# Moving chunk 2's input and the norm weights from SyncE's DMA queue to ScalarE's in a one-core hybrid decoder layer

## The chip, the cores and the metric

The kernel runs on one core of one Trainium2 chip. The metric is the time of one execution on the device in microseconds (us), lower is better. Each engine of the core (TensorE or PE, VectorE or DVE, ScalarE or ACT, GpSimd or POOL, SyncE or SP) works through its own list of instructions in order; the lists meet through semaphores. A DMA is started by an instruction in the list of one engine.

## The reference

One layer of a decoder on 1024 prompt tokens and 64 sample tokens that share all weights, in float32:

```
x = x + 0.5 * rms(swiglu_1(rms(x, n1a)), n1b)      # up: 1024 -> 2 x 2816, down: 2816 -> 1024
z = rms(x, mxa) @ w_in
a = sliding-window attention with sinks;  b = short conv + gated DeltaNet, gated rms
m = (sigmoid(gA) * (a @ w_a) + sigmoid(gB) * (b @ w_b)) @ w_out
x = x + rms(m, mxb)
x = x + 0.5 * rms(swiglu_2(rms(x, n2a)), n2b)
rms(v, w) = v * rsqrt(mean(v * v) + 1e-6) * w
```

Only the first few tens of microseconds of the first SwiGLU matter here: `silu(h @ gate) * (h @ up)` with `h = rms(x, n1a)`.

## The kernel before

Everything lies feature-major: 1024 features are 8 tiles `k` of 128 partitions, tokens are columns. The 1088 tokens are cut into three chunks of 384, 384 and 320 columns; chunk 2 holds the last 256 prompt tokens and the 64 sample tokens. Every float32 matrix is split into a rounded high part and a remainder (names `h_` and `l_` for weights, `xuh`/`xul`, `xsh`/`xsl` for inputs), and a product is three matmuls: high by high (line 142), high by remainder (143), remainder by high (144). For a weight piece of 128x512 the high part is a cast on ScalarE (line 115), the remainder a subtraction on VectorE (line 116). Weight pieces arrive in buffers named `r_` (4 of them) and `q_` (3); a buffer is free again when VectorE has made the remainder.

The kernel begins with chunk 2 alone (`pass_a`): for hidden tiles f = 0, 1, 2, ... it multiplies by the gate and the up weight. `first()` loads the four weight pieces of f = 0 (`r_w`), each followed by a quarter of chunk 2's input (`load_x(2, ...)`, two tiles k: 128 x 640), then the identity and the ones (`eye1`). `make_xn` scales the input by the norm weight (`vec`) and splits it: `xuh` on ScalarE (line 202), `xul` on VectorE (line 203). The statistic of the norm (`stat(2)`, the function `rms`) runs beside it: squares on ScalarE (line 170), sums on VectorE (lines 172 and 175), a matmul with ones (line 179, tile `po`), then ScalarE and VectorE make the factor `r`. In group 0 (f = 0 to 3) the factor is applied behind the matmuls (lines 388 to 391); from group 1 on the matmuls read `xs`, which is scaled by it beforehand (`make_xnr`: line 215 on VectorE, 195 on ScalarE, 196 on VectorE). Between the hidden tiles, `input1` fetches chunks 0 and 1 and makes their statistics (`po_725` for chunk 0), and `ldd` fetches the down weights (`h_da`), whose products are added up in `ya` (lines 347 to 351).

The code is not the order of execution. A scheduler in the framework sorts the instructions of every engine when the kernel is built, by data dependences, by priorities (`high_priority` raises one) and by its own estimates of when data is there; what comes out is fixed and each engine then keeps it. So a DMA that moves to another engine's list can change the order of the rest. In the kernel before, every DMA is issued by SyncE.

Of the kernel before, what the change touches and what calls it, by code (L numbers as in the profile page):

```python
# [35 lines left out]
def body(ctx: ExitStack, tc: tile.TileContext, d):  # L36
    nc = tc.nc
# [8 lines left out]

    eye1 = cp.tile([P, 2 * P], F32, tag="eye1", name="eye1")
    vec = cp.tile([P, V_END], F32, tag="vec", name="vec")
    nc.sync.dma_start(vec, d["vec"])
    ident = eye1[:, 0:P]  # L50
    ones = eye1[:, P : 2 * P]

    def width(c):
        return CH[c][1] - CH[c][0]
# [13 lines left out]
    def whole(pool, c, name, dt=F32):  # L68
        return [pool.tile([P, 4, width(c)], dt, tag="big", name=f"{name}{c}_{j}") for j in range(2)]

    def at(t, k):
        return t[k // 4][:, k % 4, :]

    def pair(pool, c, name):
        return whole(pool, c, f"{name}h", F32R), whole(pool, c, f"{name}l", F32R)

    def f32(ap):
        return ap.bitcast(F32)
# [3 lines left out]
    def uid(s):  # L82
        cnt[0] += 1
        return f"{s}_{cnt[0]}"
# [25 lines left out]
    def raw(name):  # L110
        return wp.tile([P, 4, P], F32, tag="raw", name=f"r_{name}", bufs=4)

    def split_w(full, hi, lo):
        with tc.high_priority(offset=20000):
            nc.scalar.copy(hi, full)  # L115
            nc.vector.tensor_tensor(out=lo, in0=full, in1=f32(hi), op=ALU.subtract)
        return hi, lo

    def slot(name, pool=wp, tag="w"):
        return (  # L120
            pool.tile([P, 4, P], F32R, tag=f"{tag}h", name=f"h_{name}"),
            pool.tile([P, 4, P], F32R, tag=f"{tag}l", name=f"l_{name}"),
        )
# [40 lines left out]
    def rms(pool, src, n, dst, scale, urgent=False):  # L164

        t = pool.tile([P, 4, 384], F32, tag="big", name=uid("rms"))
        acc, sq = t[:, 0:2, :n], t[:, 2:4, :n]
        for k in range(0, KT, 2):
            for i in range(2):
                nc.scalar.activation((sq if k else acc)[:, i, :], src(k + i), AF.Square)  # L170
            if k:
                nc.vector.tensor_tensor(out=acc, in0=acc, in1=sq, op=ALU.add)
            yield
        one, ve = acc[:, 0, :], acc[:, 1, :]
        nc.vector.tensor_tensor(out=one, in0=one, in1=ve, op=ALU.add)
        yield
        ps = po_tile()
        with tc.high_priority(offset=4000 if urgent else 0):
            sums.append(nc.tensor.matmul(ps[:, :n], ones, one, start=True, stop=True))
        nc.scalar.activation(dst, ps[:, :n], AF.Abs_reciprocal_sqrt, scale=scale, bias=epsc)  # L180
        nc.scalar.activation(ve, ps[:, :n], AF.Identity, scale=scale, bias=epsc)
        newton(dst, ve, one)
        yield

    def drain(steps):
        for _ in steps:
            pass

    def take(steps, n):
        for _ in range(n):  # L190
            if next(steps, steps) is steps:
                return
# [5 lines left out]
    def make_xn(x, xn, wcol):  # L198
        xh, xl = xn
        for k in range(KT):  # L200
            wv = vec[:, wcol + k : wcol + k + 1]
            nc.scalar.activation(at(xh, k), at(x, k), AF.Copy, scale=wv)
            nc.vector.scalar_tensor_tensor(
                out=at(xl, k), in0=at(x, k), scalar=wv, in1=f32(at(xh, k)), op0=ALU.mult, op1=ALU.subtract
            )
            if k % 2:
                yield

    def make_xnr(x, xn, wcol, rr, c):

        xh, xl = xn
        n = width(c)
        for k in range(KT):
            t = t2()[:, :n]
            nc.vector.scalar_tensor_tensor(
                out=t, in0=at(x, k), scalar=wcol[:, k : k + 1], in1=rr, op0=ALU.mult, op1=ALU.mult
            )
            split(t, at(xh, k), at(xl, k))
            if k % 2:
                yield  # L220
# [25 lines left out]
    def spill(y, dst):  # L246
        for j in range(2):
            nc.sync.dma_start(dst[:, 4 * j : 4 * j + 4, :], y[j])

    def scaled(x, wcol, rr):  # L250

        for k in range(KT):
            nc.vector.scalar_tensor_tensor(
                out=at(x, k), in0=at(x, k), scalar=wcol[:, k : k + 1], in1=rr, op0=ALU.mult, op1=ALU.mult
            )
            if k % 2:
                yield
# [284 lines left out]
    def rtile(name, c):  # L542
        return cp.tile([P, width(c)], F32, tag=f"r{c}", name=f"{name}{c}")
# [3 lines left out]
    def unit(u, name):  # L547
        return load_w(win[u], name)
# [5 lines left out]
    with tc.tile_pool(name="f1", bufs=12, side="left", reuse_waits="tile") as big1, tc.tile_pool(  # L554
        name="d1", bufs=4, side="right", reuse_waits="tile"
    ) as dw1:
        r1 = [rtile("r1", c) for c in range(3)]
        x0 = [whole(xp, 0, "x0"), whole(xp, 1, "x0"), whole(big1, 2, "x0")]
        xu = pair(xp, 2, "xu")

        def load_x(c, k):
            nc.sync.dma_start(x0[c][k // 4][:, k % 4 : k % 4 + 2, :], d[f"x{c}"][:, k : k + 2, :])

        def stat(c):
            return rms(big1, lambda k: at(x0[c], k), width(c), r1[c], 1.0 / 1024.0, False)

        def first():
            ws = []
            for i in range(2):
                for w in range(2):  # L570
                    t = raw(f"w0{w}{i}")
                    nc.sync.dma_start(t, d["up1"][w * NFF][:, 4 * i : 4 * i + 4, :])
                    load_x(2, 4 * i + 2 * w)
                    ws.append(split_w(t, *slot(f"w0{w}{i}")))
            nc.sync.dma_start(eye1, d["eye1"])
            drain(make_xn(x0[2], xu, V_N1A))
            with tc.high_priority(offset=20000):
                drain(stat(2))
            return ws[0::2], ws[1::2]

        f1 = FFN(d["up1"], d["dn1"], Two(big1, dw1), "a")
        xs2 = []
        cx1 = {}

        def input1():
            for c in range(2):
                for k in range(0, KT, 2):
                    load_x(c, k)
                yield
                yield from stat(c)  # L590
                yield from scaled(x0[c], hn1, r1[c])
            yield from combine(big1, x0[0], x0[1], cx1)

        def xs1(g):
            if g == 1 and not xs2:
                xs2.append(pair(big1, 2, "xs"))
                drain(make_xnr(x0[2], xs2[0], hn1, r1[2], 2))
            return xs2[0] if g else xu

        xn2 = [None] * 3  # L600
        r2 = [None] * 3
        xd1 = [d[f"x{c}"] for c in range(3)]

        def again(src, wcol, rr):
            x = whole(xp, 2, uid("xk"))
            for j in range(2):
                nc.sync.dma_start(x[j], src[:, 4 * j : 4 * j + 4, :])
            xs = pair(xp, 2, uid("xk"))
            drain(make_xnr(x, xs, wcol, rr, 2))
            return xs  # L610

        def close1(c):
            y = f1.y[c]
            yield from post(big1, y, hv1, xd1, c, early=True)
            xn2[c] = pair(xp, c, "xb")
            r2[c] = rtile("r2", c)
            spill(y, xd[c])
            if c == 2:
                yield from make_xn(y, xn2[c], V_MXA)
                yield from rms(big1, lambda k: at(y, k), width(c), r2[c], 1.0 / 1024.0)  # L620
            else:
                yield from rms(big1, lambda k: at(y, k), width(c), r2[c], 1.0 / 1024.0)
                yield from make_xnr(y, xn2[c], hnx, r2[c], c)

        def both(close):
            yield from close(0)
            yield from close(1)

        early, late = input1(), both(close1)

        def before(g, i):
            if g or i > 1:
                take(early, 3)
            if (g, i) == (CUT - 1, 3):
                drain(early)

        f1.run(xs1, cx1, lambda: again(d["x2"], hn1, r1[2]), before, lambda g, i: (g, i) != (CUT, 0) and take(late, 4), r=lambda g: None if g else r1[2], first=first)
        drain(late)
        wk = unit(U_K, "k")
        drain(close1(2))  # L640
        behind = sums[-2:]

        nc.sync.dma_start(wabr, d["wab"])
        nc.scalar.copy(wab[:, :, 0:8], wabr)
        nc.vector.tensor_tensor(out=wab[:, :, 8:16], in0=wabr, in1=f32(wab[:, :, 0:8]), op=ALU.subtract)
# [1056 lines left out]
```

## Time and profile before

| what | value |
|---|---|
| time, median of 3 runs | 2398.41 us (2397.77 to 2401.87) |
| the profiled execution: its time, and the span of its trace | 2392.79 us, 2390.9 us |
| granted TensorE clock | 0.995 |
| TensorE busy | 2344.9 us, 98% of the span |
| VectorE, ScalarE busy | 71%, 47% |
| DMA | 276 MB, 116 GB/s over the span |

A row of the timeline reads: start (us from the span's start), length, engine, line of the kernel, operation, output tile <- input tiles, sizes, number of merged instructions, and in brackets how long the engine had been idle before and what ended that. A row of the table of windows gives, for a stretch of time, the busy time of each engine with its instructions, the granted clock, the share of time in which the 16 DMA engines were busy, and the GB/s that they moved. SPq is the queue in which SyncE issues DMAs; a row there is the issue, not the transfer.

### The profile page before, as it was taken

What the parts mean: (1) busy time and instruction counts of PE and PEld (TensorE: products, weight loads), DVE (VectorE), ACT (ScalarE), POOL (GpSimd) and SP (SyncE); (2) the same over time, 40 slices, a digit from 0 to 9 for tenths busy, and PEclk for the clock granted to TensorE, in tenths of its full rate; (3) what the DMA queues carried; (4) which work ended last, traced back from release to release, by engine and by line L of the source; (5) the groups of instructions that cost most, each with busy time, mean ns of one, the idle gap of its engine ahead of it and who ended that gap; (6) DMA issues with size and microseconds to landing.
All of it is one profiled execution on the core that took longest, in us unless ns stands there. A gap on an engine that the chain in (4) does not pass through costs nothing. (4 is left out here: it accounts for less than half of the span.)

```text
span 2390.9 us, 38846 instructions
## 1 busy us (share of the span) xinstructions
PE 2344.9 (98%) x14535; PEld 2286.1 (96%) x14535; DVE 1697.5 (71%) x3453; ACT 1112.6 (47%) x2314; POOL 21.0 (1%) x21
## 2 busy tenths in 40 slices
PE   8999999999999999999999999999999999999997
PEld 7999999999999988899899999999999999999997
DVE  8887667677688567675598456588877667677677
ACT  7644323333366455552564453367644323333344
POOL 0000000000000000000000000000000000000000
PEclk9999999999999999999999999999999999999998
DMA  8332212212464420424322346456432212212453
GB/s 276 120 115 88 69 57 83 67 63 84 162 192 140 168 78 32 138 65 132 96 94 78 111 153 196 145 191 217 127 115 85 71 58 81 70 63 84 160 170 129
DMA packets 173828, 276.19 MB, mean 116 GB/s; under 512 B 35276, under 2 KB 76208, under 8 KB 173632
## 3 DMA queue, kind: packets, MB, share of 16 engines
q1 hardware_dynamic: 173640, 273.71, 35.9%
q8 instruction: 114, 1.87, 0.3%
q14 instruction: 74, 0.61, 0.1%
HBM read 231.22 MB, written 43.41 MB: 115 GB/s over the span
## 5 line engine op out<-in xcount | busy, mean ns | idle before, releaser
L466 PE MATMUL pa<-ch,h_c_s 128*128 128x384 f32 x704 | 236.4, 336 | 1.9 <-DVE t L472 1.6
L468 PE MATMUL pa<-ch,l_c_s 128*128 128x384 f32 x704 | 235.4, 334 | 0.0
L467 PE MATMUL pa<-cl,h_c_s 128*128 128x384 f32 x704 | 235.2, 334 | 0.0
L472 DVE TENSOR_TENSOR t<-pa,t 128x384 f32<-128x384 f32 x308 | 170.6, 554 | 88.6 <-PE pa L468 88.4
L466 PE MATMUL pa<-ch,h_c_a 128*128 128x384 f32 x528 | 177.1, 335 | 0.5 <-DVE t L472 0.3
L468 PE MATMUL pa<-ch,l_c_a 128*128 128x384 f32 x528 | 176.7, 335 | 0.0
L467 PE MATMUL pa<-cl,h_c_a 128*128 128x384 f32 x528 | 176.6, 334 | 0.0
L115 ACT CAST h_c_a<-r_c_a 128x512 fp32r<-128x512 f32 x132 | 81.8, 620 | 128.0 <-PE pa L467 110.7
L466 PEld LDWEIGHTS pa<-ch,h_c_s 128*128 128x128 f32 x704 | 132.2, 188 | 5.2 <-DVE t L472 5.0
L115 ACT CAST h_c_s<-q_c_s 128x512 fp32r<-128x512 f32 x132 | 82.0, 622 | 108.5 <-PE pa L467 95.4
L467 PEld LDWEIGHTS pa<-cl,h_c_s 128*128 128x128 f32 x704 | 132.2, 188 | 0.0
L468 PEld LDWEIGHTS pa<-ch,l_c_s 128*128 128x128 f32 x704 | 132.2, 188 | 0.0
L142 PE MATMUL pa<-xbh,h_ga 128*128 128x384 f32 (+1 forms) x384 | 129.1, 336 | 0.0
L144 PE MATMUL pa<-xbh,l_ga 128*128 128x384 f32 (+1 forms) x384 | 126.1, 328 | 0.0
L143 PE MATMUL pa<-xbl,h_ga 128*128 128x384 f32 (+1 forms) x384 | 126.0, 328 | 0.0
L466 PEld LDWEIGHTS pa<-ch,h_c_a 128*128 128x128 f32 x528 | 99.1, 188 | 1.5 <-DVE t L472 1.0
L467 PEld LDWEIGHTS pa<-cl,h_c_a 128*128 128x128 f32 x528 | 99.1, 188 | 0.0
L468 PEld LDWEIGHTS pa<-ch,l_c_a 128*128 128x128 f32 x528 | 99.1, 188 | 0.0
L115 ACT CAST h_c_s<-r_c_s 128x512 fp32r<-128x512 f32 x44 | 27.4, 622 | 148.8 <-PE pa L467 139.2
L142 PE MATMUL pa<-xbh,h_qkv 128*128 128x384 f32 (+1 forms) x288 | 95.2, 331 | 0.0
L144 PE MATMUL pa<-xbh,l_qkv 128*128 128x384 f32 (+1 forms) x288 | 93.9, 326 | 0.0
L143 PE MATMUL pa<-xbl,h_qkv 128*128 128x384 f32 (+1 forms) x288 | 93.9, 326 | 0.0
(627 smaller groups left out, 7253.5 us busy)
## 6 DMA issues: line engine op xcount, KB each, us to landing
r_c_a<-in_up_dram SPq DMA_DIRECT2D x132, 256.0 KB
r_wo<-in_wo_dram SPq DMA_DIRECT2D x48, 256.0 KB
q_c_a<-in_up_dram SPq DMA_DIRECT2D x44, 256.0 KB
q_ub<-in_up_dram SPq DMA_DIRECT2D x44, 256.0 KB
r_ub<-in_up_dram SPq DMA_DIRECT2D x44, 256.0 KB
r_ua<-in_up_dram SPq DMA_DIRECT2D x42, 256.0 KB
q_ua<-in_up_dram SPq DMA_DIRECT2D x42, 256.0 KB
r_da<-in_dn_dram SPq DMA_DIRECT2D x40, 256.0 KB
```

Source lines behind the costliest of these rows:

```text
L115: nc.scalar.copy(hi, full)
L142: nc.tensor.matmul(ps[:, :n], hi[:, j, :], at(xh, k), start=first, stop=False)
L143: nc.tensor.matmul(ps[:, :n], hi[:, j, :], at(xl, k), start=False, stop=False)
L144: mm = nc.tensor.matmul(ps[:, :n], lo[:, j, :], at(xh, k), start=False, stop=last)
L466: nc.tensor.matmul(ps, wh[:, k, :], xh[:, k, :], start=k == 0, stop=False)
L467: nc.tensor.matmul(ps, wh[:, k, :], xl[:, k, :], start=False, stop=False)
L468: nc.tensor.matmul(ps, wl[:, k, :], xh[:, k, :], start=False, stop=k == 3)
L472: nc.vector.tensor_tensor(out=out, in0=ps, in1=other, op=ALU.add)
```

## The change

The DMAs of the norm weights and of the four quarters of chunk 2's input are issued by ScalarE in place of SyncE. SyncE's list so begins with the first weights. Nothing is computed otherwise.

```
-    nc.sync.dma_start(vec, d["vec"])
+    nc.scalar.dma_start(vec, d["vec"])
...
         def load_x(c, k):
-            nc.sync.dma_start(x0[c][k // 4][:, k % 4 : k % 4 + 2, :], d[f"x{c}"][:, k : k + 2, :])
+            (nc.scalar if c == 2 else nc.sync).dma_start(x0[c][k // 4][:, k % 4 : k % 4 + 2, :], d[f"x{c}"][:, k : k + 2, :])
```

The built lists of TensorE, VectorE, ScalarE and SyncE differ over the first 500 to 900 TensorE instructions, and not behind that. SyncE's list now begins with the four `r_w`, `eye`, and the weights of f = 1, where each `r_w` stood ahead of a quarter of the input. ScalarE's list before, from the cast of the first weight piece on (`h_w` are the weights of f = 0, `h_ua` those of the following f, `x_0` and `x_1` the two halves of chunk 2's input):

```order
L115 CAST h_w_145<-r_w_142 128x512
L202 ACTIVATE xuh_0_135<-x_0_133,vec 128x320 x2
L115 CAST h_w_152<-r_w_149 128x512
L170 ACTIVATE rms_187<-x_0_133 128x320 x4
L115 CAST h_w_159<-r_w_156 128x512
L202 ACTIVATE xuh_0_135<-x_0_133,vec 128x320
L170 ACTIVATE rms_187<-x_1_134 128x320 x2
L115 CAST h_w_166<-r_w_163 128x512
L202 ACTIVATE xuh_0_135<-x_0_133,vec 128x320
L202 ACTIVATE xuh_1_136<-x_1_134,vec 128x320
```

ScalarE's list now, from the issue of the second quarter on; ahead of these rows stand the issue of `vec`, the load of an activation table, a one-column instruction (`seed`), the issue of the first quarter and the casts of the first two weight pieces:

```order
L562 DMA x_0_133<-in_x_dram 128x640
L115 CAST h_w_159<-r_w_156 128x512
L115 CAST h_w_166<-r_w_163 128x512
L562 DMA x_1_134<-in_x_dram 128x640
L170 ACTIVATE rms_187<-x_0_133 128x320 x4
L115 CAST h_ua_0_267<-r_ua_0_265 128x512
L115 CAST h_ua_1_273<-q_ua_1_271 128x512
L170 ACTIVATE rms_187<-x_1_134 128x320 x2
L115 CAST h_ua_0_279<-r_ua_0_277 128x512
L115 CAST h_ua_1_285<-q_ua_1_283 128x512
L562 DMA x_1_134<-in_x_dram 128x640
L202 ACTIVATE xuh_0_135<-x_0_133,vec 128x320 x4
```

The first `xuh`, which the first matmul reads, stood behind one cast; now it stands behind eight casts, six squares and all four issues of the input, and the last quarter is issued just ahead of it. TensorE's list before, around the statistic's matmul (`po_200`):

```order
L142 MATMUL pa_289<-xuh_0_135,h_ua_0_267 128x320
L143 MATMUL pa_289<-xul_0_137,h_ua_0_267 128x320
L144 MATMUL pa_289<-xuh_0_135,l_ua_0_268 128x320
L179 MATMUL po_200<-rms_187,eye_72 128x320
L142 MATMUL pa_289<-xuh_0_135,h_ua_0_267 128x320
L143 MATMUL pa_289<-xul_0_137,h_ua_0_267 128x320
```

And now:

```order
L142 MATMUL py_208<-xuh_0_135,h_w_152 128x320
L179 MATMUL po_200<-rms_187,eye_72 128x320
L143 MATMUL py_208<-xul_0_137,h_w_152 128x320
L144 MATMUL py_208<-xuh_0_135,l_w_153 128x320
L142 MATMUL pa_207<-xuh_0_135,h_w_145 128x320
L143 MATMUL pa_207<-xul_0_137,h_w_145 128x320
```

It stood behind 35 matmuls, when some of f = 1 were through already; now it stands behind 16, and it needs the squares of the last quarter. Further on, where group 1 begins, ScalarE's list before around the factor for chunk 0 (`po_725`) reads:

```order
L644 CAST wab<-wabr 128x8x8
L195 CAST xsh_0_554<-t_29_562 128x320
L180 ACT_TABLE_LOAD
L180 ACTIVATE r_126<-po_725,epsc 128x384
L195 CAST xsh_0_554<-t_30_566 128x320
L195 CAST xsh_0_554<-t_31_570 128x320
L181 ACTIVATE rms_434<-po_725,epsc 128x384
L148 ACTIVATE rms_434<-r_126 128x384
L115 CAST h_ua_0_926<-r_ua_0_924 128x512
L195 CAST xsh_1_555<-t_32_574 128x320
```

And now:

```order
L351 COPY ya_0_139<-py_691 128x320
L180 ACT_TABLE_LOAD
L180 ACTIVATE r_126<-po_725,epsc 128x384
L181 ACTIVATE rms_434<-po_725,epsc 128x384
L148 ACTIVATE rms_434<-r_126 128x384
L115 CAST h_da_707<-q_da_705 128x512
L115 CAST h_ua_1_752<-q_ua_1_750 128x512
```

All eight `xsh` now stand ahead of the table load, and behind it follows the cast of a down weight, `h_da_707`, that before had been made some twenty rows earlier.

## The prediction

> **What bounds the kernel now.** I read the page first, then who TensorE waited for at the start, then the timeline of the first 65 us.
>
> ```profile
> span 2390.9 us, 38846 instructions
> PE 2344.9 (98%) x14535; PEld 2286.1 (96%) x14535; DVE 1697.5 (71%) x3453; ACT 1112.6 (47%) x2314; POOL 21.0 (1%) x21
> ```
>
> TensorE is busy for 98% of the span, so whatever delays its list is paid in full, and the whole reserve is the 46 us in which it stands. The change is confined to the start. There TensorE's waits (waited for: us in total, times, longest) up to 150 us are:
>
> ```profile
> PE pa L142 <- ACT xuh L202: 6.1, 1, 6.1
> PE pa L142 <- ACT xsh L195: 2.7, 2, 1.7
> PE pa L142 <- ACT t L384: 0.9, 1, 0.9
> PE pa L143 <- DVE xsl L196: 0.5, 1, 0.5
> PE pa L143 <- DVE xul L203: 0.4, 1, 0.4
> ```
>
> The first 6.1 us are the wait for the first `xuh`, that is for weights, input and `vec`; 4.1 us (2.7, 0.9, 0.5) come later, where group 1 begins. The timeline shows how the first wait is made up:
>
> ```profile
> 0.74 1.28 ACT L155 ACT_TABLE_LOAD   x1 [0.74 <-PEq L1677]
> 0.75 0.39 SPq L49 DMA_DIRECT2D vec<-in_vec_dram  x1
> 1.20 0.42 SPq L572 DMA_DIRECT2D r_w<-in_up_dram  x1
> 1.66 0.43 SPq L562 DMA_DIRECT2D x<-in_x_dram  x1
> 2.04 0.20 ACT L155 ACTIVATE seed<-epsc 128x1 f32<-128x1 f32 x1
> 4.56 0.62 ACT L115 CAST h_w<-r_w 128x512 fp32r<-128x512 f32 x1 [1.85 <-DMA r_w<-in_up_dram]
> 5.45 1.01 ACT L202 ACTIVATE xuh<-x,vec 128x320 fp32r<-128x320 f32 x2 [0.27 <-DMA x<-in_x_dram]
> 6.06 0.63 PE L142 MATMUL pa<-xuh,h_w 128*128 128x320 f32 x1 [6.06 <-ACT xuh L202]
> 6.88 1.66 ACT L170 ACTIVATE rms<-x 128x320 f32<-128x320 f32 x4
> 8.18 0.47 PE L142 MATMUL pa<-xuh,h_w 128*128 128x320 f32 x1
> 8.45 0.47 PE L143 MATMUL pa<-xul,h_w 128*128 128x320 f32 x1
> 8.57 0.82 DVE L172 TENSOR_TENSOR rms<-rms 128x640 f32<-128x640 f32 x1 [0.87 <-ACT rms L170]
> 8.96 0.62 ACT L115 CAST h_w<-r_w 128x512 fp32r<-128x512 f32 x1 [0.43 <-DMA r_w<-in_up_dram]
> 13.44 0.31 PE L142 MATMUL pa<-xuh,h_w 128*128 128x320 f32 x1
> 13.59 0.31 PE L143 MATMUL pa<-xul,h_w 128*128 128x320 f32 x1
> 14.41 0.48 DVE L175 TENSOR_TENSOR rms<-rms 128x320 f32<-128x320 f32 x1
> 15.06 0.70 PE L179 MATMUL po<-rms,eye 128*128 128x320 f32 x2
> 16.62 1.01 DVE L203 SCALAR_TENSOR_TENSOR xul<-x,vec,xuh 128x320 fp32r<-128x320 f32 x2
> 17.51 0.62 ACT L115 CAST h_ua<-q_ua 128x512 fp32r<-128x512 f32 x1
> 18.03 0.62 ACT L115 CAST h_ua<-r_ua 128x512 fp32r<-128x512 f32 x1
> ```
>
> The first weight piece lands 3.36 us after its issue (1.20 to 4.56), the first `xuh` starts at 5.45, the first matmul 0.61 us behind it. ScalarE takes 0.52 us from cast to cast (17.51 to 18.03), 0.42 us for a square (1.66 for four). Early matmuls start 0.27 us apart, later ones 0.147 (13.44 to 13.59).
>
> ```profile
> 0.00:7.00 7.00, 0.94 (x2) 0.64 (x3) 2.30 (x11) 4.06 (x9) 0.21 (x4) 1.00 0.65 195
> 0.00:12.00 12.00, 5.82 (x19) 4.62 (x20) 6.17 (x17) 8.63 (x19) 0.21 (x4) 1.00 0.81 276
> ```
>
> 1.37 MB (7 us at 195 GB/s) have moved by 7 us and 3.31 MB by 12. The third weight piece, which ends 1.50 MB of issued data (57.5, 256, 320, 256, 320 and 256 KB), lands at 8.96. So landings, not issue times, set the pace.
>
> **The issues themselves.** SyncE is rid of five issues of about 0.43 us, and the four weight pieces are issued 0.45 to 1.9 us earlier. The five cost ScalarE five times that, since it keeps its list in order; no row has an issue on ScalarE, so I take SyncE's 0.43. The first quarter of the input is issued later: behind `vec` (0.39), the table load (1.28) and `seed` (0.20), at about 0.75 + 1.87 = 2.6 us in place of 1.66.
>
> **The first matmul.** The new order decides this. Ahead of the first `xuh` ScalarE now has eight casts (4.2 us), six squares (2.5) and three more issues (1.3), 8.0 us of work. It can't begin before the first weight piece, now issued 0.45 us earlier, lands at about 4.1. Lower bound: 4.1 + 8.0 + 0.61 = 12.7 us. But most of these wait for data. The fourth weight piece is behind about as many bytes as the third was (four pieces, `vec`, one quarter and half of another, which share the engines: 1.6 MB), so it lands at about 8.9. Behind it come its cast (0.52), the issue of the third quarter (0.43, at 9.4), four squares (1.66) and two casts (1.04), to 12.55; then the squares of the third quarter, which lands 3.36 us after its issue, at 12.8 to 13.2; two squares (0.83), two casts (1.04), the last issue (0.43) and 0.61 to the matmul: 15.7 to 16.1. A shorter landing than 3.36 (two rows of the weights share their queue) takes some off; I take **15.6 us** in place of 6.06. Upper bound 17, where the fourth piece lands another 1.4 us later.
>
> **The wait for `po`.** The last quarter is issued at about 15.0, lands at 18.4; two squares (0.83), a sum (0.82), one `xul` (about 0.5) and the last sum (0.48) end at 21.0. TensorE reaches `po` after 16 matmuls of 0.27 and the wait for the first `xul` (0.5), at 20.4. It waits 0.6 us; bounds 0 and 2.6 (the last quarter 2 us later, behind the copy of a cache that SyncE's list now holds at that place).
>
> **What comes off.** Before, the first `xs` matmul is the 211th of TensorE's list:
>
> ```profile
> 42.27 0.56 PE L142 MATMUL pa<-xsh,h_ua 128*128 128x320 f32 x2 [0.98 <-ACT xsh L195]
> 50.15 0.71 PE L142 MATMUL pa<-xsh,h_ua 128*128 128x320 f32 x3 [1.73 <-ACT xsh L195]
> 62.77 0.41 PE L142 MATMUL pa<-xsh,h_ua 128*128 128x320 f32 x1 [0.85 <-ACT t L384]
> ```
>
> So 210 matmuls took from 6.06 to 41.29, 35.2 us, where 210 times 0.147 is 30.9: 4.3 us went into half-speed matmuls, `po` and small waits. Now, by the steps above: 18 slow matmuls at 0.12 us extra (2.2), `po` (0.70 less 0.15), its wait (0.6), 3.3 us. The list is then 15.6 - 6.06 - 1.0 = **8.5 us late** at that point. The rows at 8.18 and 8.45 show the slow pace under a granted clock of 1.00 in the window's row, so I count it from the matmuls. The Trainium skill ("TensorE: Matmul & The Clock Gate", the section on the HAM clock gate) has the array at half rate until it was busy for about 3.4 us; the trace shows 8.45, 2.4 us in, still slow and 13.44 fast, which agrees. By the page's 3.4 us the 18 slow ones would be 13, and the sum 0.6 us smaller.
>
> Then the three waits above and the 0.5 of the table of waits, 4.1 us, are to go. With TensorE 8.5 us later against weights that are fetched as soon as buffers come free, ScalarE and VectorE reach `xs` earlier in TensorE's list, and the eight `xs` tiles stand there in a row: per pair two scalings, two casts and two subtractions, 1.9 us, where TensorE has about 5 us of other matmuls ahead and 0.9 us per tile. I take all 4.1; bounds 2 and 4.1.
>
> **A new wait.** Behind `po_725` ScalarE must now do in a row what lay apart before:
>
> ```profile
> 50.11 1.28 ACT L180 ACT_TABLE_LOAD   x1
> 51.54 0.58 ACT L180 ACTIVATE r<-po,epsc 128x384 f32<-128x384 f32 x1
> 53.20 0.52 ACT L148 ACTIVATE rms<-r 128x384 f32<-128x384 f32 x1
> 54.24 0.55 DVE L149 TENSOR_TENSOR rms<-rms 128x384 f32<-128x384 f32 x1
> 54.70 0.69 DVE L116 TENSOR_TENSOR l_ua<-r_ua,h_ua 128x512 fp32r<-128x512 f32 x1
> 65.21 0.43 ACT L351 COPY ya<-ph 128x320 f32<-128x320 f32 x1
> 76.74 0.91 PE L179 MATMUL po<-rms,eye 128*128 128x384 f32 x2
> ```
>
> From the last `py_691` matmul: copy (about 0.4), table load 1.28, three activations (0.47 apiece without the pipeline's tail), the cast of `h_da_707`: it is there at 3.6 us, its remainder, behind two VectorE steps of the norm, at 4.75. TensorE has `po_725` (0.75 to the next start) and 12 matmuls (1.76), then two more: it waits 1.1 and 0.75, together **1.9 us**. Bounds 0 and 3. Nothing behind this wants data earlier than its order has them: VectorE's lists run in step again some 270 matmuls later.
>
> **Sum.** 8.5 + 1.9 - 4.1 = 6.3 us against the profiled execution's 2392.79, 2399.1. That execution lies 5.6 us under the median of the three; on the median, 2398.41 + 6.3 = **2404.7 us**. Least: first matmul at 12.7 (5.6 late), no new wait, all 4.1 regained: +1.5, 2399.9. Most: 17 us (9.9 late), 2 more at `po`, 1.9, 2 regained: +11.8, 2410.2.
>
> **Rivals.** No change, the data is early: two queues feed the same engines, weights and input land as ScalarE asks, and only its 8 us of work count. Against it: DMA is already busy for 0.81 of the first 12 us. It gives the +1.5 above with the new wait gone, or +3.4 with it; under 0.2% (4.8 us, about what a measurement here can tell from no change) either way. No change, only issue times matter: the first quarter is issued 0.9 us later and TensorE starts at 7.0, about 2399.3. The Trainium skill's rule ("DMA: Bandwidth & Descriptors", Issuing engines are not separate DMA queues) gives this one: that issuing from several engines only saves the time to issue. For it the trace has that landings set the pace; against it stands that ScalarE's list is in order, so what is issued there moves compute too. Faster: the input lands so soon that the first matmul beats 6.06, with all later waits gone. It needs 15.6 to become 6.0 or less (then -1.1 - 4.1 = -5.2, 2393.2); the lower bound of 12.7 rules it out unless the casts are far quicker than 0.52. Slower still: the last quarter is held up behind the cache copy and the input of chunks 0 and 1 follow late, so that `po` waits 2.6 and the `xs` waits stay half: 2398.4 + 8.5 + 2.0 + 1.9 - 2.0 = 2408.8.
>
> **How the numbers follow.** My forecast 0.54, slower still 0.13, early data 0.21, issue times only 0.08, faster 0.04. By sign: slower by over 0.2% 0.67, within 0.2% 0.29, faster 0.04. Range: from 2400.5 (early data with most of its cases) to 2409.5 (just over slower still); the likeliest case alone runs from 2402 to 2407.
>
> **What would show it.** First matmul at 15 to 16 us, released by `xuh`; ScalarE's idle time ahead of that ended by DMAs of `r_w` and `x`; `po` waiting under 1 us for line 175; no waits for `xsh`; a wait of 1 to 2 us for `h_da` behind `po_725`; from about 150 us on the same rows as before, 6 us later. I am wrong if the first matmul comes before 13 us, or if the waits for `xs` return.

## The result, and the profile after

The changed kernel takes 2407.24 us (median of 19 runs, 2399.83 to 2411.01), the kernel before, beside it, 2395.55 us (19 runs, 2391.85 to 2401.87). The ratio over all runs is 1.0044, with a 95% interval from 1.0037 to 1.0050: 10.5 us slower, 8.9 to 12.0 (the two medians differ by 11.7). The prediction had +6.3 us.

The profiled execution of the changed kernel is the fastest of the 19: 2399.83 us, a span of 2397.8 against 2390.9 before. So the two traces differ by only 6.9 us, and places and amounts below are read from the first 150 us of the traces, the total from the medians. The head of the page:

```profile
span 2397.8 us, 38852 instructions
...
PE 2342.1 (98%) x14535; PEld 2286.1 (95%) x14535; DVE 1697.6 (71%) x3453; ACT 1111.7 (46%) x2314; POOL 21.0 (1%) x21
```

TensorE's waits up to 150 us (waited for: us in total, times, longest):

```profile
PE pa L142 <- ACT xuh L202: 15.1, 1, 15.1
PE ph L347 <- ACT h_da L115: 2.2, 1, 2.2
PE pa L142 <- ACT xsh L195: 1.7, 1, 1.7
PE po L179 <- DVE rms L175: 0.8, 2, 0.5
PE ph L349 <- DVE l_da L116: 0.7, 1, 0.7
```

Against the five rows of before: the first wait is 15.1 in place of 6.1; the rows for `t` and `xsl` are gone; `xsh` has kept 1.7 of its 2.7; and there are 2.2 + 0.7 us for `h_da` and its remainder. The timeline of the start (ACTq is the queue in which ScalarE issues DMAs):

```profile
0.75 0.41 ACTq L49 DMA_DIRECT2D vec<-in_vec_dram  x1
...
1.19 1.28 ACT L155 ACT_TABLE_LOAD   x1 [1.19 <-PEq L1677]
1.26 0.39 ACTq L562 DMA_DIRECT2D x<-in_x_dram  x1
...
4.01 0.62 ACT L115 CAST h_w<-r_w 128x512 fp32r<-128x512 f32 x1 [1.33 <-DMA r_w<-in_up_dram]
...
5.21 0.33 ACTq L562 DMA_DIRECT2D x<-in_x_dram  x1
...
6.20 1.29 ACT L115 CAST h_w<-r_w 128x512 fp32r<-128x512 f32 x2 [0.38 <-DMA r_w<-in_up_dram]
...
6.88 0.36 ACTq L562 DMA_DIRECT2D x<-in_x_dram  x1
...
10.27 0.83 ACT L170 ACTIVATE rms<-x 128x320 f32<-128x320 f32 x2 [2.04 <-DMA x<-in_x_dram]
...
12.69 0.47 ACT L170 ACTIVATE rms<-x 128x320 f32<-128x320 f32 x1 [0.57 <-DMA x<-in_x_dram]
12.85 0.33 ACTq L562 DMA_DIRECT2D x<-in_x_dram  x1
...
14.46 1.92 ACT L202 ACTIVATE xuh<-x,vec 128x320 fp32r<-128x320 f32 x4
...
15.07 0.63 PE L142 MATMUL pa<-xuh,h_w 128*128 128x320 f32 x1 [15.07 <-ACT xuh L202]
...
17.86 0.83 ACT L170 ACTIVATE rms<-x 128x320 f32<-128x320 f32 x2 [1.49 <-DMA x<-in_x_dram]
...
19.20 0.44 PE L143 MATMUL pa<-xul,h_w 128*128 128x320 f32 x1
...
20.47 0.81 PE L179 MATMUL po<-rms,eye 128*128 128x320 f32 x2 [0.52 <-DVE rms L175]
```

What the reader is to see: the issue at 1.26 runs beside the table load, and the third and fourth weight pieces are cast in a row at 6.20. ScalarE waits for the input: 2.04 us ahead of 10.27, 0.57 ahead of 12.69, 1.49 ahead of 17.86. The second to fourth quarters land 5.0 to 5.8 us after their issue (5.21 to 10.27, 6.88 to 12.69, 12.85 to 17.86), where the first weight piece took 3.3 (0.75 to 4.01).

The second place is where group 1 begins. TensorE's rows of the timeline there:

```profile
50.44 0.56 PE L142 MATMUL pa<-xsh,h_ua 128*128 128x320 f32 x2 [1.74 <-ACT xsh L195]
...
66.23 0.42 PE L347 MATMUL ph<-ha,h_da 128*128 128x320 f32 x1 [2.22 <-ACT h_da L115]
...
67.51 0.64 PE L349 MATMUL ph<-ha,l_da 128*128 128x320 f32 x1 [0.72 <-DVE l_da L116]
67.94 0.47 PE L347 MATMUL ph<-ha,h_da 128*128 128x320 f32 x1
...
70.34 0.47 PE L142 MATMUL pa<-xsh,h_ua 128*128 128x320 f32 x1
```

ScalarE's rows of the same stretch:

```profile
62.91 1.28 ACT L180 ACT_TABLE_LOAD   x1
...
65.56 0.62 ACT L115 CAST h_da<-q_da 128x512 fp32r<-128x512 f32 x1
```

And the table of windows (the granted clock is the third figure from the right):

```profile
66.00:68.00 2.00, 1.05 (x4) 0.79 (x5) 1.97 (x5) 1.73 (x4) 0.00 (x0) 0.82 0.00 0
68.00:70.00 2.00, 2.00 (x9) 2.00 (x9) 2.00 (x4) 1.03 (x2) 0.00 (x0) 0.50 0.68 219
```

The cast of `h_da_707` stands behind the table load, as the order had shown, and TensorE waits 2.22 us for it and 0.72 for its remainder. Then comes what before shows nowhere in its first 150 us: the granted clock falls from 1.00 to 0.50, and the ten matmuls from 67.94 to 70.34 start 0.27 us apart in place of 0.147. That costs another 1.2 us.

### The profile page after: what moved, and what is told of

It is laid out like the page before. It is cut to its first block, busy times and chain, and to the rows that moved or that the text cites. A ratio compares the mean times of both kernels' runs of the same rounds, so it can differ in the third digit from the quotient of the medians.

```text
span 2397.8 us, 38852 instructions
## 1 busy us (share of the span) xinstructions
PE 2342.1 (98%) x14535; PEld 2286.1 (95%) x14535; DVE 1697.6 (71%) x3453; ACT 1111.7 (46%) x2314; POOL 21.0 (1%) x21
## 3 DMA queue, kind: packets, MB, share of 16 engines
q8 instruction: 114, 1.87, 0.3%
## 4 chain that ended last, share of the span: by engine, by line
PE 84%; DVE 8%; ACT 4%; DMA 3%; issue 1%; SPq 0%; DVEq 0%; ACTq 0%
PE pa L142 11%; PE pa L143 11%; PE pa L144 10%; PE pa L466 8%; PE pa L468 8%; PE pa L467 8%; PE ph L349 4%; PE ph L348 4%; PE ph L347 4%; PE py L349 4%; PE py L348 4%; PE py L347 4%; DVE t L875 1%; ACT s L821 1%; DMA q_da<-in_dn_dram 1%
```

## The experiments

Every list of TensorE has the same number of matmuls, so a trace gives for each kernel how late the nth matmul starts against the trace of before (where the lists differ, it need not be the same matmul). This table, in us, is worked out from the start times (n counted from 1); the kernels are explained below it. It also has the time against before by the ratio of the runs, times 2396 us, with its interval.

| kernel | 1st | 121st | 211th | 301st | 501st | time against before |
|---|---|---|---|---|---|---|
| the change | +9.0 | +8.3 | +10.3 | +10.1 | +9.6 | +10.5 (8.9 to 12.0) |
| the change again | +9.8 | +8.8 | +11.4 | +11.9 | +12.2 | +11.7 (7.9 to 15.6) |
| vec_only | -0.5 | +1.0 | +1.0 | -0.2 | -0.2 | +2.6 (0.2 to 5.3) |
| x_only | +8.2 | +7.9 | +9.7 | +5.2 | +8.5 | +15.3 (12.0 to 18.7) |
| queue_only | +2.3 | +1.8 | +5.9 | +5.3 | +7.6 | +12.5 (9.1 to 15.8) |
| queue_sp | 0.0 | -0.5 | -0.5 | -0.5 | -0.1 | +3.4 (0.5 to 6.0) |
| order_only | +9.9 | +8.3 | +8.3 | +6.1 | +4.7 | +5.3 (2.9 to 7.4) |
| before_sp | 0.0 | -0.1 | +1.6 | +8.2 | +10.0 | +12.0 (8.4 to 15.8) |
| after_sp | +9.9 | +12.1 | +12.1 | +9.8 | +10.1 | +10.1 (6.5 to 13.7) |
| after_hda | +9.0 | +8.7 | +13.3 | +9.6 | +9.5 | +12.7 (8.6 to 16.5) |
| pool_both | +5.6 | +4.0 | +4.0 | +1.4 | +0.3 | +3.8 (1.7 to 6.2) |
| stat_late | 0.0 | -0.1 | -0.1 | -3.1 | -4.3 | -0.5 (-3.6 to 2.4) |
| stat_late2 | -0.1 | -0.2 | +0.3 | -4.2 | -4.2 | +15.1 (11.7 to 18.4) |

Several kernels hold a list in a given order by edges that only order instructions of one engine and wait for nothing:

```
+    def chain(*steps):
+        for a, b in zip(steps, steps[1:]):
+            tc.add_manual_dep(b.ins, a.ins.name, NOSYNC, reason="order")
```

**Each half of the change alone.**

```
-    nc.sync.dma_start(vec, d["vec"])
+    nc.scalar.dma_start(vec, d["vec"])
```

> Only the norm weights are issued by ScalarE; the input stays with SyncE. TensorE's and VectorE's lists are then word for word those of before, ScalarE's has one issue more at its head. Order theory (the time follows from what stands ahead of the first xuh in ScalarE's list): first matmul at 6.0 us, time as before within 1.5 us. Queue theory (two issuing engines make the transfers land later): vec lands later than 2.6 us and the first xuh may wait for it, but the first xuh starts at 5.45 anyway, so 0 to 1 us. Both near zero: this run says whether the input alone is to be looked at.

At the 501st matmul it is level. The time is 2398.48 us (11 runs) against 2396.45, ratio 1.0011 (1.0001 to 1.0022): 2.6 us, over the 1.5 expected, by an interval that begins at 0.2.

```
-            nc.sync.dma_start(x0[c][k // 4]...
+            (nc.scalar if c == 2 else nc.sync).dma_start(x0[c][k // 4]...
```

> Only the input is issued by ScalarE; vec stays with SyncE. ScalarE's list has the same eight casts, six squares and four issues ahead of the first xuh as in the changed kernel, but the cast of the down weight h_da_707 stands ahead of the table load for po_725. Order theory: first matmul at 14 to 15.5 us, 8 us late at the 200th matmul, no wait for h_da and no stretch of half clock behind it, so 4.1 us better than the changed kernel: before + 5 to 6.5 us. Queue theory: the same start, and the same end as the changed kernel, before + 9 to 10.5.

The start came as expected (14.2 us, 7.9 late at the 121st), and no wait for `h_da`. Both theories had the end wrong: 2410.71 us, ratio 1.0064 (1.0050 to 1.0078), worse than the whole change. From the 211th matmul on it waits at other places; two rows of TensorE's waits up to 150 us:

```profile
PE pa L142 <- ACT xsh L195: 1.4, 1, 1.4
PE pa L142 <- ACT h_ua L115: 1.4, 1, 1.4
```

So the wait for `h_da` is not the one thing that keeps the late start from being regained: with the same late start and another later order, other waits do it. What it loses behind the 501st matmul (9.8 late at the 1001st, 11.7 at the 4001st) was not followed up; the next runs hold the lists.

**The queues alone.** vec and input issued by ScalarE as in the change, ScalarE's list held as before, with the four issues of the input ahead of its first cast:

```
+            chain(*issues[:4], casts[0], *xuhs[:2], casts[1], *squares[:4], casts[2], xuhs[2],
+                  *squares[4:6], casts[3], xuhs[3], xuhs[4], *squares[6:8], casts[4], ..., casts[7])
```

> The queues of the changed kernel, but ScalarE's casts, squares and xuh are held in the order of before by edges that order and do not wait, and the four issues of the input stand ahead of the first cast. Order theory: the first matmul comes at 5.5 to 7.5 us and the time is that of before within 3 us, either way. Queue theory: SyncE's and ScalarE's transfers share the engines and all land late, first matmul at 9 us or later, before + 3 us or more.

The first matmul came at 8.4, between the two theories, and the time rose by 12.5 us, which looked like the queue theory. The timeline of its start shows what differs besides the queues:

```profile
0.75 1.81 SPq L580 DMA_DIRECT2D r_w<-in_up_dram  x4
...
3.93 3.30 ACTq L570 DMA_DIRECT2D x<-in_x_dram  x2
...
4.10 2.10 SPq L136 DMA_DIRECT2D q_ua<-in_up_dram  x3
...
7.28 0.62 ACT L121 CAST h_w<-r_w 128x512 fp32r<-128x512 f32 x1 [4.60 <-DMA r_w<-in_up_dram]
...
8.28 0.72 SPq L807 DMA_DIRECT2D out_kso_dram<-in_kc_dram  x1
...
9.13 3.45 SPq L136 DMA_DIRECT2D r_ua<-in_up_dram  x3
```

The scheduler had SyncE fetch three pieces (`q_ua`, 4.10) and a copy of a cache (8.28) ahead of the three `r_ua` at 9.13, with weights for f = 1 among them. The first weight piece, issued at 0.75, was cast only at 7.28. The row puts this down to a weight piece, but all four issues of the input stand ahead of that cast in ScalarE's list, and the last two ran only between 3.93 and 7.23. By the semaphores in the trace, the DMAs of SyncE and ScalarE use eight semaphores in turn, and an issue that takes one over waits until the earlier DMA on it has landed: the third issue of the input waited for the first weight piece (until 3.91), the fourth for the third piece (until 6.88). So an issue in ScalarE's list can hold up the casts behind it. This run doesn't tell queue from order, and its repetition holds SyncE's list too:

```
+    chain(heads[0], *wl[:8], *xs_[0], *wl[8:20], *xs_[1], *wl[20:31], late_[0], wl[32], ...)
```

(`heads` is the identity, `wl` the weight pieces from f = 1 on in the order of the code, `xs_` the input by chunk, `late_` the projection `wabr` and the two cache copies.)

> The queues of the changed kernel alone: ScalarE issues vec and the four quarters of the input ahead of its first cast, and the lists of ScalarE and of SyncE are both held in the order of before (in the run of the queues before this one SyncE still fetched five more pieces and two copies of a cache ahead of the weights of f = 1). Order theory, now of both lists: first matmul at 5.5 to 7.5 us, no new wait from 20 to 60 us, time as before within 3 us. Queue theory (two issuing engines): the first weights share the DMA engines with the whole input, first matmul at 8 us or later, and before + 3 us or more.

Three rows of its timeline:

```profile
4.09 0.82 ACTq L571 DMA_DIRECT2D x<-in_x_dram  x2
...
4.96 0.62 ACT L122 CAST h_w<-r_w 128x512 fp32r<-128x512 f32 x1 [2.27 <-DMA vec<-in_vec_dram]
...
6.09 0.63 PE L149 MATMUL pa<-xuh,h_w 128*128 128x320 f32 x1 [6.09 <-ACT xuh L209]
```

The first matmul comes at 6.09 against 6.06, and up to the 501st the kernel is level with before (-0.1 us). The order theory held that far; the time is 1.0014 (1.0002 to 1.0025). The Trainium skill ("DMA: Bandwidth & Descriptors", Issuing engines are not separate DMA queues) says that issuing from several engines saves only the time to issue. By these rows even that saving did not reach TensorE: the weights were issued from 0.75 on in place of 1.20, but the first cast came at 4.96 (before 4.56). Its row names `vec`, which the cast doesn't read. Ahead of the cast in ScalarE's list stand the third and fourth issue of the input, which ran from 4.09 to 4.91; the third takes over the semaphore of `vec` and waited until that had landed (4.07).

**ScalarE's order, all DMAs on SyncE.** SyncE issues everything; ScalarE's list is held in the order of the change:

```
+            chain(*casts[:4], *squares[:4], *casts[4:6], *squares[4:6], *casts[6:8],
+                  *xuhs[:4], *squares[6:8], *xuhs[4:8])
```

> The queues of before (SyncE issues everything), but ScalarE's list is held in the order of the changed kernel: eight casts and six squares ahead of the first xuh. Order theory: the eighth weight piece, behind some 3.4 MB, lands at about 12 us, first matmul at 13 to 15 us, 7 to 8 us late at the 200th matmul, later waits partly regained: before + 3 to 6 us. Queue theory: the first matmul stays at 6 to 8 us and the time within 1.5 us of before.

The first matmul comes at 15.9 us: the order alone makes the late start, with the queues untouched. But 3.6 of the 8.3 us are regained by the 501st, the regain that the prediction had counted on, and the time is 1.0022 (1.0012 to 1.0031), +5.3 us, half of what the change costs. TensorE does not wait for `h_da` here, so those waits don't follow from ScalarE's order at the start by itself. The lists behind the start were not held in this run: from its 19th DMA on the scheduler sorted SyncE's list anew too, with chunk 1's input between the weights as in the change.

**SyncE's order, the start as before.** The start is as before, and SyncE's list is held in the order of the change from the weights of f = 1 on (the chain above with another sequence, worked out from the list of the changed kernel). after_sp is the mirror: the start of the change, with SyncE's list as before, held from the weights of f = 2 on.

> The mirror: all DMAs issued by SyncE and the start as before, but SyncE's list from the weights of f = 1 on held in the order of the changed kernel. The scheduler then gives ScalarE the eight xsh in a row, and h_da_707 behind the table load for po_725, as in the changed kernel. Theory (two losses): first matmul at 6 us, within 1 us at the 120th, then waits for xsh and h_da, 4 to 8 us late at the 500th matmul, time before + 4 to 8. Rival (that order costs only when the start is late): within 2 us of before throughout.

TensorE's rows of its timeline, with the wait in brackets:

```profile
62.30 0.64 PE L353 MATMUL ph<-ha,h_da 128*128 128x320 f32 x1 [7.00 <-ACT h_da L121]
...
65.62 0.63 PE L355 MATMUL ph<-ha,l_da 128*128 128x320 f32 x1 [2.42 <-DVE l_da L122]
```

ScalarE's row between the table load (55.00) and the cast of `h_da` (61.63):

```profile
59.63 2.10 ACT L281 CAST ch<-x 128x384 fp32r<-128x384 f32 x4 [1.87 <-DVE x L259]
```

Its table of windows there:

```profile
56.00:60.00 4.00, 0.00 (x0) 0.00 (x0) 2.14 (x4) 2.12 (x5) 0.00 (x0) 0.67 0.00 0
60.00:64.00 4.00, 0.90 (x2) 0.50 (x2) 4.00 (x8) 3.95 (x9) 0.00 (x0) 0.50 0.00 0
```

And the longest wait of SyncE's queue from 20 to 70 us:

```profile
SPq L343 <- DVE l_da L122: 22.2, 1, 22.2
```

So the order behind the start costs time without any late start. With the start on time, the order in which SyncE fetches, and the order that the scheduler then gives ScalarE (the two were not tried apart), make TensorE wait 7.00 and 2.42 us for `h_da` and its remainder at the 293rd and 295th matmul, the same places as in the change, and halve the clock: 10.0 us late at the 501st matmul, time 1.0050 (1.0035 to 1.0066). The expectation of 4 to 8 was too low. It is more than the change's 2.22 and 0.72 at these places, mainly because ScalarE's list is not quite that of the change: there the cast of `h_da_707` follows the factor directly, here four casts of chunk 0's input (59.63) stand between, and ScalarE waits 1.87 us for VectorE ahead of them. The late start and this order cost 5.3 and 12.0 us apart and 10.5 together, so they don't add up, and how much of the 10.5 belongs to each is not shown.

The row of SyncE's queue is its wait, 22.2 us in one piece, for a buffer that is free only when the remainder `l_da` is made: that weight's cast stands behind the table load on ScalarE, and until then nothing more is fetched. In the changed kernel the longest such wait is 22.5 us.

> The changed kernel, with SyncE's list held in the order of before from the weights of f = 1 on. The start stays that of the changed kernel (eight casts, six squares and four issues ahead of the first xuh); behind it the scheduler then gives ScalarE nearly the list of before again, without eight xsh in a row and with h_da_707 far ahead of the table load. Theory (two losses: the late start, most of which is regained, and SyncE's order from f = 1 on): first matmul at 15 us, 8.3 us late at the 200th matmul, regained to 4 to 5.5 us late at the 500th, time before + 4 to 6. Rival (the late start alone is the loss and is not regained): 8 us late or more at the 500th, time as the changed kernel.

Half as expected. The `h_da` wait is gone and 2.0 us are regained from the 121st to the 501st matmul. But the start became worse, 12.1 us late in place of 8.3. SyncE now issues chunk 0's input (1.6 MB) just as ScalarE issues the last quarter, as its timeline shows:

```profile
13.49 1.87 SPq L568 DMA_DIRECT2D x<-in_x_dram  x4
...
13.69 0.34 ACTq L568 DMA_DIRECT2D x<-in_x_dram  x1
...
20.35 0.83 ACT L176 ACTIVATE rms<-x 128x320 f32<-128x320 f32 x2 [3.08 <-DMA x<-in_x_dram]
...
22.95 1.44 PE L185 MATMUL po<-rms,eye 128*128 128x320 f32 x2 [1.85 <-DVE rms L181]
```

That quarter lands 6.7 us after its issue (13.69 to 20.35; 5.0 in the change) and `po` waits 1.85. That the input beside it is the reason is likely, but not tried apart. The time, 1.0042 (1.0027 to 1.0057), is that of the change; the mirror doesn't separate the two halves cleanly.

**The one wait.** The changed kernel with one edge more:

```
+        tc.add_manual_dep(facts[1].ins, downs["a", 0, 3].ins.name, NOSYNC, reason="order")
```

(`facts[1]` is the first activation of the factor for `po_725`, `downs["a", 0, 3]` the cast of `h_da_707`.)

> The changed kernel with one edge more: ScalarE makes the cast of h_da_707 ahead of the table load and the factor for po_725, not behind them. The start is the same word for word. Theory (this one place costs 2.2 + 0.7 us of waiting and 1.2 us of half clock behind it): no wait for h_da, granted clock 1.00 throughout 60 to 80 us, 4.1 us less than the changed kernel. Rival (the wait only stands in for the lag of ScalarE and VectorE, which ends in another wait a little later): 0 to 2 us less.

The rival held. The wait for `h_da` is gone and the clock stays at 1.00 there, but the wait for `xsh` is 3.7 us in place of 1.7, with the half clock behind it. ScalarE's row of its timeline ahead of that place:

```profile
37.03 0.62 ACT L117 CAST h_da<-r_da 128x512 fp32r<-128x512 f32 x1 [4.89 <-DMA r_da<-in_dn_dram]
```

TensorE's row:

```profile
52.77 0.90 PE L144 MATMUL pa<-xsh,h_ua 128*128 128x320 f32 x2 [3.68 <-ACT xsh L197]
```

And the window behind it:

```profile
54.00:56.00 2.00, 2.00 (x9) 2.00 (x9) 1.94 (x5) 0.74 (x2) 0.00 (x0) 0.50 0.03 8
```

Up to that place both lists are alike; here a down weight landed late, and ScalarE stood 4.89 us for it (2.90 at the same cast in the first trace of the change). Nothing was gained by the 501st matmul, and the time is 1.0053 (1.0036 to 1.0069).

> The changed kernel once more, for a second trace beside that of the fastest of its runs. Theory (the later stages vary from execution to execution in how often the clock is halved, the first 150 us do not): first matmul at 15 us and the waits for h_da (2.2 and 0.7) again, 9 to 10 us late at the 4000th matmul, and other stretches of half clock behind 1000 us than the first trace. Rival (the change itself slows the later stages): the lag against before grows by several us behind the 4000th matmul in this trace and not in that of the kernels that share its start.

The two waits for `h_da` came back at 2.2 and 0.5 us and that for `xsh` at 1.8; the lag is 12.2 us at the 501st matmul and still 12.2 at the 4001st. The first trace had 9.6 at both. So the changed kernel loses 9.6 to 12.2 us in its first 100 us, and in neither trace does the lag grow from there to the 4001st matmul. That the first 150 us don't vary was wrong: they differ by 2.6 us. Most of that difference is the clock. In this trace it was halved behind the wait for `xsh` too, where the first trace stayed at 1.00, and behind `h_da` the half clock lasted 6.8 us in place of 3.4:

```profile
50.98 0.76 PE L142 MATMUL pa<-xsh,h_ua 128*128 128x320 f32 x2 [1.79 <-ACT xsh L195]
...
52.00:54.00 2.00, 2.00 (x10) 2.00 (x9) 1.94 (x6) 0.52 (x2) 0.00 (x0) 0.50 0.03 8
```

**Another engine for the issues, and a candidate.** GpSimd's list is empty at the start; the two lines read `nc.gpsimd` in place of `nc.scalar`:

> vec and the input issued by GpSimd, whose list is empty there, in place of ScalarE; nothing held. ScalarE's list then has four casts and four squares ahead of the first xuh, and TensorE's po at its 29th place. Order theory: the first matmul waits for the fourth weight piece (6.8 to 8 us), one cast, two squares and the xuh: 9 to 11 us, and the time is between before and the changed kernel, before + 2 to 7. Queue theory (the engine that issues matters, not the order): as the changed kernel, before + 9 to 11.

The order theory held: the time is 1.0016 (1.0007 to 1.0026), +3.8 us. The first matmul comes at 11.6 us, later than the 9 to 11 expected, since ScalarE's list holds four casts and four squares ahead of the first `xuh` and the fourth piece comes late (its cast at 9.79 waits 0.81 us for it). Yet of these 5.6 us 0.3 are left at the 501st: the start by itself costs little where the later lists add no waits, since TensorE before has 4.1 us of waits in that stretch. Three kernels that are level with before at the 501st matmul (this one, vec_only, queue_sp) nonetheless come out 2.6 to 3.8 us slower, by intervals that begin at 1.7, 0.2 and 0.5. In their single traces the lag grows later (queue_sp is 5.5 us late at the 4001st matmul, vec_only 6.9 at the 8001st), where stretches of half clock come that the trace of before lacks. Whether these belong to the kernels or to the executions is not shown.

The candidate takes work out of the stretch in which before's later waits lie, on before's queues:

```
-            if g or i > 1:
+            if g:
                 take(early, 3)
```

> A candidate on the kernel before, queues untouched: the input of chunks 0 and 1 and their statistics begin one group later (group 1 in place of f = 2 of group 0), which takes eight squares of ScalarE and four sums of VectorE out of the stretch from 35 to 60 us, where TensorE waits for xsh, t and xsl (4.1 us in all). Theory (there ScalarE and VectorE are the limit, so less work there is time): 2 to 4 us less than before. Rival (the same work comes due a little later and TensorE waits there instead, or chunk 0 is not ready in time): 0, or some us more than before.

It is 5.5 us ahead at the 331st matmul, more than the theory had, and 8.1 us behind at the 1001st: in between, the longest of TensorE's waits are 4.5 us for `ch`, the high part of chunk 0's input, which is scaled by the factor from that statistic. With half the step (`i > 2`):

> The same candidate with half the step: the input of chunks 0 and 1 and their statistics begin at f = 3 in place of f = 2, not a group later. Theory (the crowded stretch of ScalarE and VectorE around group 1 is the limit, and a smaller shift doesn't make chunk 0 late): 2 to 5 us ahead of before at the 330th to 400th matmul, and no more than 2 us of that lost by the 1000th, time before - 1 to - 4. Rival (what leaves that stretch comes due before pass 2 whatever the step): level with before or behind it at the 1000th matmul, time before - 1 to + 5.

It is 4.3 us ahead at the 501st matmul and 2.1 at the 1001st, between the two expectations; the time is 2395.47 us against 2395.85 (ratio 0.9998, 0.9985 to 1.0010), no gain that can be measured. No kernel of this study beats before.

## Why the prediction was right in direction and 4 us short

- **First x issue at 2.6 us, behind the table load.** This was wrong: it came at 1.26. ScalarE's queue issued while the table load ran (1.19 to 2.47).
- **First matmul at 15.6.** It came at 15.07 (15.8 in the second trace), but was composed otherwise. The fourth weight piece was there by 6.8 and not 8.9, and the third quarter was issued at 6.88 and not 9.4; landings of 5.0 to 5.8 us in place of 3.36 took that back. That the two errors cancelled is luck. The step that the order decides the start held (order_only 15.9, queue_sp 6.09).
- **`po` waits 0.6.** It waited 0.52.
- **16 to 18 slow matmuls.** There were 14 by the spacing (from the first to the one at 19.20), so the 18 times 0.12 was too much by 0.5. The 13 that the prediction worked out from the Trainium skill's 3.4 us ("TensorE: Matmul & The Clock Gate", What's actually happening) were nearer.
- **8.5 us late at the first `xs` matmul.** It was 8.3, and 8.8 in the second trace: this term was right.
- **All 4.1 us of later waits gone.** This is the term that was mis-sized first: `t` (0.9) and `xsl` (0.5) went, `xsh` kept 1.7 of 2.7, so 2.4 was regained. The reason given, that ScalarE and VectorE would reach `xs` earlier because TensorE is late, overlooked that their own data came later: SyncE's list is no longer that of before, and ScalarE stood 2.90 us for a down weight 15 us ahead of that place. In after_hda, where that wait was 4.89, the first `xsh` was cast 2.3 us later (52.25 against 49.92). The prediction had named the return of the waits for `xs` as a sign that it is wrong; by that sign this step failed.
- **A new wait of 1.9.** It was placed rightly, but was 2.9 us (2.2 + 0.7), near the upper bound of 3. ScalarE made three copies of `ya` in a row ahead of the table load (61.82 to 62.91) where one was counted, and the half clock that came behind the pause (1.2 us) had no term.
- **Sum.** 8.3 - 2.4 + 2.9 + 1.2 = 10.0, against 9.4 measured at the 331st matmul, behind the last of before's waits (at its 317th), and 9.6 at the 501st; the forecast was 8.5 - 4.1 + 1.9 = 6.3. Direction and range held. The forecast time, 2404.7, lies only 2.5 us under the measured 2407.24, but that is luck in part: the median that it started from, 2398.41, lay 2.9 us above the 2395.55 measured beside the change.
- **"From about 150 us on the same rows, 6 us later."** They were about 10 us later, and from the 501st to the 4001st matmul the lag does not move.
- **Rivals.** "Issue times only" is what the queues do by themselves as far as the 501st matmul (queue_sp is level there); the change cost time because it re-sorts lists. "Early data" had the weights right, which were early, but the input was not. "Slower still" had the size (2408.8) but only half of the mechanism: `po` did not wait 2.6, but 1.7 of the 4.1 us of later waits stayed, near the half that it said.

## What to carry to other kernels

Where a scheduler sorts the lists, moving a DMA to another engine's queue is a change of order first: compare all lists, SyncE's too, and cost each place where a load, a cast or a copy moves past something that waits. A delay at the start is worth only what the later waits don't take up (in pool_both 5.3 of 5.6 us were gone 500 matmuls later), so look at the next place where TensorE waits, and at what order the weights for it are fetched in. An issue is also an entry in a list: what stands behind it waits with it (in queue_only a cast stood until 7.28 behind an issue that waited for another DMA). A pause of TensorE of about 3 us cost here its own length and 1.2 us of half clock in one trace, and twice that half clock in the other.

## What was not expected of the hardware

- **The clock after a pause.** A pause of 2.22 us, two matmuls and 0.72 us more brought half clock (0.50 in the row 68 to 70 of the change); the pause of 1.74 us (50.44) did not, nor did 1.85 in after_sp or 2.8 for `t` in queue_only; 3.68 in after_hda and 7.00 in before_sp did. But in the second trace of the change the pause of 1.79 us at the same place (50.98) brought it, so length alone doesn't decide. The Trainium skill ("TensorE: Matmul & The Clock Gate", What's actually happening) has the clock fall after at least one idle window of about 3.4 us, in windows that run freely; here pauses shorter than that were enough, and the same pause was or was not, from one execution to the next.
- **The same lists, not the same time.** vec_only has TensorE's list of before word for word, is level at the 501st matmul, and 6.9 us behind at the 8001st. The stretches of half clock in the middle stages come and go from execution to execution, of one and the same kernel too. A row of the table of windows of the first trace of the change, where the granted clock is 0.83:

```profile
1190.00:1200.00 10.00, 9.97 (x39) 6.97 (x39) 7.47 (x16) 2.38 (x7) 1.41 (x1) 0.83 0.48 159
```

The same row of the second trace of the change, with 1.00:

```profile
1190.00:1200.00 10.00, 9.63 (x52) 7.34 (x52) 5.93 (x13) 2.73 (x8) 3.78 (x2) 1.00 0.49 158
```

From 1685 to 1695 it is the other way round, 1.00 and 0.83. A single profiled execution so says little about 5 us in 2400.
- **Sharing.** `vec`, 57 KB, issued at 0.75 in both kernels and first on its queue in both, lands later when it is on ScalarE's queue beside four weight pieces on SyncE's. VectorE's first use of it stood at 2.62 before; in the changed kernel its row reads:

```profile
4.17 0.17 DVE L531 TENSOR_SCALAR hv<-vec 128x8 f32<-128x8 f32 x1 [3.30 <-DMA vec<-in_vec_dram]
```
